# Two-layer hybrid decoder trunk on one Trainium2 core: the 512-column matmuls of the values and of the gate's v half are written as two of 256 columns

## The chip, the cores and the metric

The kernel is one program on one core of a Trainium2 chip. The core has a matrix engine (TensorE, PE in the profile, with its weight loads shown apart as PEld), a vector engine (VectorE, DVE), a scalar engine (ScalarE, ACT), GpSimd (POOL) and SyncE (SP), which here issues the weight DMAs. The time is device microseconds (us) of the whole program on that core; one profiled execution beside the timed runs gives the trace.

## What is computed

Two layers on 256 positions of width 2048, in fp32. Cut to what matters here:

```python
for l in range(DEPTH):                                  # 2 layers
    z = rms_norm(x, norm1_g[l]) @ w_in[l]               # 2048 -> 5120
    q, k, v, gu, gv = split(z)                          # 1024 columns each
    attn = dilated_attention(rotary(q), rotary(k), v)   # 8 heads
    gm = chunked_gmlp(gelu(gu), gelu(gv), ...)          # 8 groups, chunk 128
    x = x + concat(attn, gm) @ w_out[l]                 # 2048 -> 2048
    x = x + square(relu(rms_norm(x, norm2_g[l]) @ w_up[l])) @ w_down[l]   # 2048 -> 8192 -> 2048
return rms_norm(x, final_g)
```

The values `v` and the gate's v half `gv` are the two parts of `z` that the change touches: 2 layers x 2 parts x 1024 columns.

## The kernel before

Activations and weights are fp32. Each is split into a high part, rounded to the reduced fp32 type (`fp32r`), and a low part, the rest, and each product is made of three matmuls: high by high, high by low, low by high. `hs` holds the activations after the norm's gain, both parts, with the model's columns on the partitions and the 256 positions along the free axis. Weights come in pieces (`Sub`) of 128 x 1024 fp32 (512 KB): SP loads `raw` (6 buffers), ACT makes `hi` (L160, 7 buffers), DVE makes `lo` (L170, 6 buffers).

Three functions make the matmuls.

- `transposed` (L361 to L396) makes q, k, the gate's u half, the output projection, the up projection and three quarters and more of the down projection. The stationary operand is a 128 x 128 block of weights, the moving one is 256 columns (positions) of activations. Three lines: L391 (hi by high), L393 (lo by high), L395 (hi by low). A piece is 24 matmuls.
- `fast` (L398 to L431) makes the other part of the down projection by a seven-product scheme on 2 x 2 blocks. Here the stationary operand is a 128 x 128 block of activations, the moving one is 256 columns of weights: L420, L422, L423. A step makes six products (36 matmuls) and leaves the seventh (6 matmuls) in `left_over`, which the next piece of `transposed` runs after its first three matmuls (L386).
- `natural` (L433 to L452) makes `v` and `gv`. The stationary operand is a 128 x 128 block of activations, the moving one is 512 columns of weights, and the sum over the 16 blocks of the model width fills two whole PSUM banks, one for each half of the positions (`tt`). Lines L449 (xh by hi), L450 (xh by lo), L451 (xl by hi). A piece is 12 matmuls (2 blocks of rows, 2 halves of positions, 3 products); 8 pieces make 512 columns, and two such groups make a stage of 192 matmuls. There are four stages, two in each layer: the values are the layer's first stage, and the gate's v half stands between q/k and the gate's u half. In all 768 matmuls.

After a group of 512 columns, `after_v` has ACT copy the two banks out with the norm's factor (L540); `after_gv` has ACT scale them (L636) and starts the gelu.

The order is written by hand. A loop (L901 to L921) goes through `steps`: ahead of each step's matmuls it issues the ACT and DVE work for pieces two to six steps ahead and the loads, and after them it takes work from a queue (`later`, `soon`, `hook`). Some of that work is small fp32 matmuls or transposes on PE (L305, L313, L518, L573 to L580, L606, L619, L621, L675, L778), which so stand between the matmuls of a stage.

Of the kernel before, what the change touches and what calls it, by code (L numbers as in the profile page):

```python
# [39 lines left out]
KC = D // P  # L40
# [45 lines left out]
def trunk(ctx: ExitStack, tc: tile.TileContext, layout, xT, consts, gains, w, b_sp, w_sp, out):  # L86
# [10 lines left out]
    vec, act, pe = nc.vector, nc.scalar, nc.tensor  # L97
# [29 lines left out]
    def acc_bank(i=None, of=4):  # L127

        if i is None:
            i = bank_at[0] = (bank_at[0] + 1) % of  # L130
        return pacc.tile([P, 512], F32, name=f"acc{i}", tag=f"acc{i}")
# [301 lines left out]
    def natural(name, l, col0, ncols, after):  # L433

        for c in range(0, ncols, 512):
            acc = [None]
            for k0 in range(0, KC, 2):
                wt = Sub(name, l, k0 * P, col0 + c, 2, 512)

                def mm(wt=wt, k0=k0, acc=acc):  # L440
                    if k0 == 0:
                        acc[0] = [acc_bank(), acc_bank()]
                    for k in range(2):
                        for tt in range(2):
                            xh = hs[:, k0 + k, 0, tt * P:(tt + 1) * P]
                            xl = hs[:, k0 + k, 1, tt * P:(tt + 1) * P]
                            hi, lo = wt.hi[:, k, :], wt.lo[:, k, :]
                            ps = acc[0][tt]
                            pe.matmul(ps, lhsT=xh, rhs=hi, start=(k0 + k == 0), stop=False)  # L449
                            pe.matmul(ps, lhsT=xh, rhs=lo, start=False, stop=False)  # L450
                            pe.matmul(ps, lhsT=xl, rhs=hi, start=False, stop=(k0 + k == KC - 1))  # L451
                steps.append((wt, mm, (lambda c=c, acc=acc: after(c, acc[0])) if k0 + 2 == KC else None))  # L452

    def mark(fn):
# [470 lines left out]
    n = norms[-1]  # L925
# [3 lines left out]
    for c, w in [(0, 1), (1, 1)] + [(c, 2) for c in range(2, KC, 2)]:  # L929
        r = slice(c, c + w)  # L930
# [38 lines left out]
```

## Time and profile before

| what | value |
|---|---|
| timed runs | 2041.94, 2041.50, 2038.93 us; median 2041.5 us |
| the profiled execution | 2041.88 us, of which the span of its instructions is 2040.1 us |
| PE busy | 2025.8 us (99%), 16914 matmuls |
| PEld busy | 1988.5 us (97%), 16914 weight loads |
| DVE busy | 1584.5 us (78%) |
| ACT busy | 1052.6 us (52%) |
| mean granted TensorE clock | 0.997 of full |

The profile's times are of one execution. A matmul's shown duration is longer than the time to the next one's start, since matmuls are pipelined: what a stream of them costs is the distance between starts, read from the timeline as (last start minus first start) / (number of steps between).

### The profile page before, as it was taken

The page shows a single profiled execution, that of the slowest core. Times are in us where ns is not written, and L with a number is a line of the kernel's source. Part 1 is how long each engine was busy: PE and PEld are TensorE (multiplying, and loading weights), DVE is VectorE, ACT ScalarE, POOL GpSimd, SP SyncE. Part 2 cuts the span into 40 slices and gives each one's busy share as a digit, 9 for nine tenths or more (in the row PEclk, how much of TensorE's full clock was granted, in tenths as well). Part 3 has the DMA queues.
Part 4 walks back from the last instruction along what each step waited for, and adds up shares of the span by engine and source line. Part 5 has one row for each costly group of instructions (what it writes and reads, how often), then busy time and mean ns, then how long its engine had stood idle before and what let it go on. Part 6 is the DMA issues. An engine that isn't in the chain of part 4 may idle for free.

```text
span 2040.1 us, 40532 instructions
## 1 busy us (share of the span) xinstructions
PE 2025.8 (99%) x16914; PEld 1988.5 (97%) x16914; DVE 1584.5 (78%) x1970; ACT 1052.6 (52%) x1325; POOL 68.7 (3%) x90
## 2 busy tenths in 40 slices
PE   9999999999999999999999999999999999999997
PEld 8998999999999999999989989999999999999997
DVE  7666766798888888888865667668988888888886
ACT  7565444455545455444644654544554544545444
POOL 0002300000000000000000032000000000000000
PEclk9999999999999999999999999999999999999998
DMA  8545555465565655645564455554655565556553
GB/s 318 189 166 167 186 191 201 166 218 190 195 225 167 217 196 197 217 158 215 185 232 163 166 186 187 186 198 165 209 201 200 207 207 186 199 195 212 194 191 108
DMA packets 112120, 395.39 MB, mean 194 GB/s; under 512 B 12352, under 2 KB 16448, under 8 KB 111936
## 3 DMA queue, kind: packets, MB, share of 16 engines
q1 hardware_dynamic: 110800, 389.86, 56.0%
q8 instruction: 132, 2.16, 0.4%
q10 hardware_dynamic: 1136, 2.94, 0.4%
q14 instruction: 52, 0.43, 0.1%
HBM read 390.65 MB, written 2.10 MB: 193 GB/s over the span
## 4 chain that ended last, share of the span: by engine, by line
PE 98%; DVE 2%; DMA 0%; ACT 0%; issue 0%; DVEq 0%; ACTq 0%
PE acc L393 24%; PE acc L391 24%; PE acc L395 24%; PE acc L449 3%; PE acc L451 3%; PE acc L450 3%; PE aux L422 3%; PE aux L423 3%; PE aux L420 3%; PE acc L423 2%; PE acc L422 2%; PE acc L420 2%; DVE lo L170 1%; PE aux L675 0%; PE aux L619 0%; PE aux L577 0%
## 5 line engine op out<-in xcount | busy, mean ns | idle before, releaser
L160 ACT ACTIVATE hi<-raw 128x1024 fp32r<-128x1024 f32 (+1 forms) x801 | 808.0, 1047 | 473.4 <-DVE raw L214 202.0
L170 DVE TENSOR_TENSOR lo<-raw,hi 128x1024 fp32r<-128x1024 f32 (+1 forms) x801 | 944.9, 1215 | 48.7 <-ACT hi L160 33.0
L391 PE MATMUL acc<-hs,hi 128*128 128x256 f32 x2816 | 781.1, 277 | 0.0
L393 PE MATMUL acc<-hs,lo 128*128 128x256 f32 x2816 | 778.5, 276 | 0.0
L395 PE MATMUL acc<-hs,hi 128*128 128x256 f32 x2816 | 778.3, 276 | 0.0
L391 PEld LDWEIGHTS acc<-hs,hi 128*128 128x128 f32 x2816 | 529.0, 188 | 0.4 <-issue 0.2
L393 PEld LDWEIGHTS acc<-hs,lo 128*128 128x128 f32 x2816 | 528.8, 188 | 0.6 <-issue 0.2
L395 PEld LDWEIGHTS acc<-hs,hi 128*128 128x128 f32 x2816 | 528.6, 188 | 0.0
L391 PE MATMUL acc<-half,hi 128*128 128x256 f32 x1600 | 442.7, 277 | 0.0
L395 PE MATMUL acc<-half,hi 128*128 128x256 f32 x1600 | 442.2, 276 | 0.0
L393 PE MATMUL acc<-half,lo 128*128 128x256 f32 x1600 | 442.2, 276 | 0.0
L391 PEld LDWEIGHTS acc<-half,hi 128*128 128x128 f32 x1600 | 300.8, 188 | 0.0
L393 PEld LDWEIGHTS acc<-half,lo 128*128 128x128 f32 x1600 | 300.4, 188 | 0.0
L395 PEld LDWEIGHTS acc<-half,hi 128*128 128x128 f32 x1600 | 300.3, 188 | 0.0
L629 ACT ACTIVATE half<-ar 128x512 fp32r<-128x512 f32 x72 | 45.6, 634 | 190.0 <-DVE ar L734 175.4
L489 DVE TENSOR_TENSOR x<-x,acc 128x512 f32<-128x512 f32 (+1 forms) x89 | 60.3, 677 | 68.7 <-PE acc L395 68.6
L733 DVE TENSOR_TENSOR ar<-acc,nR 128x512 f32<-128x512 f32 x64 | 44.1, 689 | 86.9 <-PE acc L395 86.9
L449 PE MATMUL acc<-hi,hs 128*128 128x512 f32 x256 | 101.5, 396 | 0.7 <-ACT hs L277 0.7
L451 PE MATMUL acc<-hi,hs 128*128 128x512 f32 x256 | 100.5, 393 | 0.0
L450 PE MATMUL acc<-lo,hs 128*128 128x512 f32 x256 | 100.1, 391 | 0.0
L630 DVE TENSOR_TENSOR half<-ar,half 128x512 fp32r<-128x512 f32 x72 | 49.9, 692 | 50.4 <-ACT half L629 50.4
L277 ACT ACTIVATE hs<-x,cols 128x256 fp32r<-128x256 f32 x64 | 29.0, 501 | 91.5 <-DVE x L489 90.3
(150 smaller groups left out, 2251.8 us busy)
## 6 DMA issues: line engine op xcount, KB each, us to landing
raw<-in_w SPq DMA_DIRECT2D x731, 512.0 KB, 4.6
raw<-in_w SPq DMA_DIRECT2D x10, 256.0 KB, 5.2
x<-in_xT SPq DMA_DIRECT2D x7, 256.0 KB, 5.6
out<-x SPq DMA_DIRECT2D x7, 256.0 KB, 3.1
shared<-in_b_sp ACTq DMA_DIRECT2D x2, 512.0 KB, 8.2
shared<-in_w_sp ACTq DMA_DIRECT2D x2, 512.0 KB, 10.4
con<-in_consts ACTq DMA_DIRECT2D x1, 512.0 KB, 7.5
x<-in_xT ACTq DMA_DIRECT2D x1, 256.0 KB, 4.2
```

Of the source, the lines that this page charges most:

```text
L160: act.activation(self.h[:, j * m:(j + 1) * m], self.raw[:, j * m:(j + 1) * m], AF.Copy)
L170: vec.tensor_tensor(lo[:, r], self.raw[:, r], self.h[:, r].bitcast(F32), op=OP.subtract)
L391: pe.matmul(o, lhsT=hi, rhs=xs[:, 0, :], start=(k0 + k == 0 and (two or cb == 0)), stop=False, skip_group_check=True)
L393: pe.matmul(o, lhsT=wt.lo[:, k, cb * P:(cb + 1) * P], rhs=xs[:, 0, :], start=False, stop=False, skip_group_check=True)
L395: pe.matmul(o, lhsT=hi, rhs=xs[:, 1, :], start=False, stop=last, skip_group_check=True)
L420: pe.matmul(o[n], lhsT=xh, rhs=hi, start=(p == 0 and k == 0 and n in fresh), stop=False, skip_group_check=True)
L422: pe.matmul(o[n], lhsT=xh, rhs=lo, start=False, stop=False, skip_group_check=True)
L423: pe.matmul(o[n], lhsT=xl, rhs=hi, start=False, stop=(last and p == 1 and k == 1), skip_group_check=True)
L449: pe.matmul(ps, lhsT=xh, rhs=hi, start=(k0 + k == 0), stop=False)
L450: pe.matmul(ps, lhsT=xh, rhs=lo, start=False, stop=False)
L451: pe.matmul(ps, lhsT=xl, rhs=hi, start=False, stop=(k0 + k == KC - 1))
L489: vec.tensor_tensor(xj, xj, ps[j][:, 0:S] if alone else pair(ps)[:, j, :], op=OP.add)
```

## The change

In `natural` the three matmuls of a block become six: each product is made for the columns 0 to 255 and then for the columns 256 to 511 of the same banks, with the same stationary operand.

```diff
-                            hi, lo = wt.hi[:, k, :], wt.lo[:, k, :]
-                            ps = acc[0][tt]
-                            pe.matmul(ps, lhsT=xh, rhs=hi, start=(k0 + k == 0), stop=False)
-                            pe.matmul(ps, lhsT=xh, rhs=lo, start=False, stop=False)
-                            pe.matmul(ps, lhsT=xl, rhs=hi, start=False, stop=(k0 + k == KC - 1))
+                            for xp, wp_, n in ((xh, wt.hi, 0), (xh, wt.lo, 1), (xl, wt.hi, 2)):
+                                for h in range(2):
+                                    r = slice(256 * h, 256 * h + 256)
+                                    pe.matmul(acc[0][tt][:, r], lhsT=xp, rhs=wp_[:, k, r],
+                                              start=(k0 + k == 0 and n == 0 and h == 0),
+                                              stop=(k0 + k == KC - 1 and n == 2), skip_group_check=True)
```

On PE, at the first block of rows of the first stage, before (rows are source line, operation, the PSUM bank written, the operands read, the shape written):

```order
L449 MATMUL acc_165<-hi,hs 128x512
L450 MATMUL acc_165<-lo,hs 128x512
L451 MATMUL acc_165<-hi,hs 128x512
L449 MATMUL acc_166<-hi,hs 128x512
L450 MATMUL acc_166<-lo,hs 128x512
L451 MATMUL acc_166<-hi,hs 128x512
```

On PE at the same place now, all six products from the one line L450:

```order
L450 MATMUL acc_165<-hi,hs 128x256 x2
L450 MATMUL acc_165<-lo,hs 128x256 x2
L450 MATMUL acc_165<-hi,hs 128x256 x2
L450 MATMUL acc_166<-hi,hs 128x256 x2
L450 MATMUL acc_166<-lo,hs 128x256 x2
L450 MATMUL acc_166<-hi,hs 128x256 x2
```

The products stand in the same order, each as a pair, and the 768 matmuls of the four stages become 1536; each has a weight load of its own, as before. On PE at the end of the first layer's gate v half, where the stage hands over to `transposed` (the gate's u half), now:

```order
L450 MATMUL acc_2171<-lo,hs 128x256 x2
L450 MATMUL acc_2171<-hi,hs 128x256 x2
L391 MATMUL acc_2462<-hs,hi 128x256
L393 MATMUL acc_2462<-hs,lo 128x256
L395 MATMUL acc_2462<-hs,hi 128x256
```

The hand-over is direct, as it was: no other PE instruction stands between the stage's last matmul and L391. The order on DVE, ACT, POOL and SP is unchanged.

## Rows read from the trace of the kernel before

**Rows 1.** Page, parts 1 and 2: engines, then 40 slices of the span

```profile
PE 2025.8 (99%) x16914; PEld 1988.5 (97%) x16914; DVE 1584.5 (78%) x1970; ACT 1052.6 (52%) x1325; POOL 68.7 (3%) x90
...
PEclk9999999999999999999999999999999999999998
```

**Rows 2.** Page, part 4: the chain that ended last, by engine

```profile
PE 98%; DVE 2%; DMA 0%; ACT 0%; issue 0%; DVEq 0%; ACTq 0%
```

**Rows 3.** Groups by line and shape: busy us, mean ns | idle before, releasers

```profile
L449 PE MATMUL acc<-hi,hs 128*128 128x512 f32 x256 | 101.5, 396 | 0.7 <-ACT hs L277 0.7
L451 PE MATMUL acc<-hi,hs 128*128 128x512 f32 x256 | 100.5, 393 | 0.0
L450 PE MATMUL acc<-lo,hs 128*128 128x512 f32 x256 | 100.1, 391 | 0.0
...
L450 PEld LDWEIGHTS acc<-lo,hs 128*128 128x128 f32 x256 | 48.1, 188 | 10.6 <-issue 0.2 <-DVE lo L170 0.2
```

**Rows 4.** By stretch: us, busy PE, PEld, DVE, ACT, POOL (x instructions), PEclk, DMA, GB/s

```profile
59.40:78.44 19.04, 19.04 (x170) 19.04 (x169) 11.46 (x16) 8.31 (x10) 0.00 (x0) 1.00 0.51 166
17.20:39.18 21.98, 21.98 (x98) 18.03 (x97) 20.60 (x23) 19.08 (x26) 2.42 (x1) 1.00 0.93 362
```

**Rows 5.** Timeline of PE, ends of a stretch of 512 columns: start us, us

```profile
17.20 0.39 PE L449 MATMUL acc<-hi,hs 128*128 128x512 f32 x1
...
39.18 0.39 PE L449 MATMUL acc<-hi,hs 128*128 128x512 f32 x1
```

**Rows 6.** Timeline of PE, L420 to L423 between L391 to L395

```profile
396.21 0.28 PE L420 MATMUL aux<-hi,half 128*128 128x256 f32 x1
...
400.30 0.28 PE L391 MATMUL acc<-hs,hi 128*128 128x256 f32 x1
...
401.36 0.28 PE L391 MATMUL acc<-hs,hi 128*128 128x256 f32 x1
```

**Rows 7.** Timeline of PE, the same hand-overs in another place

```profile
937.50 0.28 PE L420 MATMUL aux<-hi,half 128*128 128x256 f32 x1
...
941.74 0.28 PE L391 MATMUL acc<-hs,hi 128*128 128x256 f32 x1
...
942.77 0.28 PE L391 MATMUL acc<-hs,hi 128*128 128x256 f32 x1
```

**Rows 8.** A stretch of the first layer's down projection, columns as in Rows 4

```profile
917.50:989.30 71.80, 71.80 (x613) 71.80 (x612) 60.94 (x72) 36.81 (x44) 0.00 (x0) 1.00 0.57 200
```

**Rows 9.** Timeline of PE, L420 to L423 after fp32 transposes

```profile
911.55 0.55 PE L778 MATMUL acc<-con,ar 128*128 128x128 f32 x3 [0.61 <-DVE ar L768]
911.85 0.36 PE L420 MATMUL aux<-hi,half 128*128 128x256 f32 x1
912.05 0.28 PE L422 MATMUL aux<-lo,half 128*128 128x256 f32 x1
912.17 0.28 PE L423 MATMUL aux<-hi,half 128*128 128x256 f32 x1
912.29 0.28 PE L420 MATMUL aux<-hi,half 128*128 128x256 f32 x1
912.40 0.28 PE L422 MATMUL aux<-lo,half 128*128 128x256 f32 x1
912.52 0.28 PE L423 MATMUL aux<-hi,half 128*128 128x256 f32 x1
```

**Rows 10.** Timeline of PE, restarts after fp32 matmuls, at 512 and at 256 columns

```profile
42.73 0.48 PE L449 MATMUL acc<-hi,hs 128*128 128x512 f32 x1
43.05 0.40 PE L450 MATMUL acc<-lo,hs 128*128 128x512 f32 x1
...
212.42 0.37 PE L391 MATMUL acc<-hs,hi 128*128 128x256 f32 x1
212.62 0.28 PE L393 MATMUL acc<-hs,lo 128*128 128x256 f32 x1
212.74 0.28 PE L395 MATMUL acc<-hs,hi 128*128 128x256 f32 x1
```

**Rows 11.** L449 alone, in the four stages after their first fp32 interruption

```profile
42.73:51.06 8.33, 4.82 (x12) 2.23 (x12) 1.00 0.64 214
157.44:197.98 40.54, 22.20 (x56) 10.50 (x56) 1.00 0.58 193
1029.26:1064.49 35.23, 19.37 (x48) 9.00 (x48) 1.00 0.71 240
1168.68:1209.20 40.52, 22.20 (x56) 10.51 (x56) 1.00 0.56 193
```

**Rows 12.** Busy time after direct hand-overs from L451 to L391, columns as in Rows 4

```profile
198.50:211.00 12.50, 12.50 (x113) 12.50 (x112) 10.49 (x26) 7.42 (x9) 5.08 (x6) 1.00 0.47 144
1064.50:1091.50 27.00, 27.00 (x240) 26.99 (x239) 13.80 (x15) 13.33 (x16) 0.00 (x0) 1.00 0.46 154
```

## The prediction

> **What bounds the kernel now.** I read the engines' shares first, then the chain of waits, then the timeline of PE. PE is busy 99% of the span, and its clock digit is 9 in all slices but the last [rows 1]; the chain that ended last is PE for 98% and nothing else over 2% [rows 2]. So the time is the sum of the distances between PE's instructions, and an edit on PE is priced by what it does to these distances. In the touched stages PE's idle time is 0.7 us in all 768 matmuls [rows 3]: neither weights nor banks are late there. DVE is the nearest engine, 20.60 of 21.98 us busy in the first values stage, and PE still idles nowhere [rows 4]; elsewhere DVE has more room.
>
> The shown durations (some 393 ns for 512 columns) overlap, so I go by starts. In the first values stage 96 matmuls of 512 columns (8 pieces of 12) take from 17.20 to 39.18, 21.98 us or **228.96 ns each** [rows 5]. In q and k 168 matmuls of 256 columns (7 pieces of 24) take the 19.04 us of the stretch from 59.40 to 78.44, **113.33 ns each**; both stretches have the granted clock at 1.00, the 2.4 GHz level [rows 4]. Two of 256 are 226.67 ns, so a pair would be 2.29 ns shorter than the matmul that it replaces.
>
> But 256 columns have a second price. `fast`, with the operand roles of `natural` (activations stationary, weights moving), runs 36 matmuls from 396.21 to 400.30 (113.6 ns each), and then, over the hand-over to three matmuls of `transposed` and the six left over, 9 take 1.06 us, **117.8 ns each** [rows 6]. At another hand-over it is the other way round: 36 take 4.24 us (117.8) and the next 9 take 1.03 us (114.4) [rows 7]. So there is a short and a long rhythm, 4.4 ns apart. A stream keeps the one that it is in, and the hand-over from the `fast` form to the `transposed` form changes it: short to long in the first place, long to short in the second. In the stretch from 917.50 to 989.30 most of the 613 matmuls are in the long one: 71.80/613 is 117.1 ns [rows 8].
>
> **The change part by part.**
>
> *768 matmuls become 768 pairs.* All lie on the path. In the short rhythm: 768 x (2 x 113.33 - 228.96) = 768 x (-2.29) = **-1.8 us**. In the long one: 768 x (2 x 117.8 - 228.96) = 768 x 6.6 = **+5.1 us**. These are the two bounds. I take the short one: it is the price of the longest unbroken run of 256 columns that I read, the 168 of q and k.
>
> *768 more weight loads.* A load is shown as 188 ns and lies beside a matmul [rows 3]. The load unit goes from 18.03 of 21.98 us busy to the 19.04 of 19.04 that q and k show [rows 4]. Their 113.33 ns is thus a price with a load for each matmul in it, and nothing comes on top. That both halves use the same stationary operand saves nothing: L449 and L450 share theirs today, and L450 has all its 256 loads at 188 ns [rows 3].
>
> The Trainium skill, page "TensorE: Matmul & The Clock Gate", section "Back-to-back issue gap", gives the distance of warm matmuls as N/2.4 plus 2.5 ns, a fixed price for each, which speaks against any split: as an estimate, 768 x 2.5 = +1.9 us, and 2043.4 us without the hand-over price. The trace disagrees for these operands: if 512 columns are twice a stream time plus a fixed part, and 256 once, the fixed part is 2 x 113.33 - 228.96 = -2.3 ns in the short rhythm and +6.6 ns in the long one.
>
> *Restarts.* Ten times a small fp32 group stands between a stage's matmuls. The first matmul after it takes longer: 320 ns against 229 at 512 columns, 200 against 113 at 256 [rows 10], 91 and 87 more. No difference is counted: 10 x 4 ns.
>
> *The hand-over to `transposed`.* Three of the stages end directly before L391 (both gate v halves, and the second layer's values; the first layer's values end before a small fp32 group). If the new form acts as `fast` does, a stream that comes in short goes on long [rows 6] until the next fp32 group. After the first gate v half that is the 113 matmuls of the stretch from 198.50, and as many in the second layer; after the second values 240 [rows 12]. Today these run at the short price (27.00 us for 240 counted). 466 x 4.4 ns = **+2.1 us**; the other bound is 0.
>
> *Waits and other engines.* The wait for `hi` stays on the first matmul of a piece, that for `lo` on the first of the lo product, and the last read of each buffer is at the same place in the piece, so ACT and DVE get their buffers back as before. The banks are complete one matmul start plus a shorter matmul later: the pair's second half starts 113 ns after the first and ends where the old one ended, within some ns. Cost nothing either way; ACT's copies run beside later matmuls. Nothing moves on the DMA queue.
>
> Sum: -1.8 + 2.1 = +0.3 us. On the profiled execution's 2041.88 us (span 2040.1 and 1.8 us around it) that is 2042.2; the profiled execution lies 0.4 us over the median of the runs, 2041.5, and I predict against the median: **2041.8 us**.
>
> **The rivals.**
>
> *The gain stays, no hand-over price.* For it: today's hand-overs from L451 to L391 do not leave the long rhythm behind [rows 12]. Against: they are of 512 columns. -1.8: 2039.7 us.
>
> *Long after each restart.* After the fp32 transposes that end at 911.85, `fast` goes on at (912.52 - 912.05)/4 = 117.5 ns [rows 9]; q, k and the u half fall back to the short rhythm in three matmuls [rows 10]. `natural` has the operand roles of `fast`. L449 has 12 + 56 + 48 + 56 = 172 matmuls after the first restart of their stages [rows 11], so 3 x 172 = 516 pairs would be long and 252 short: 516 x 6.6 - 252 x 2.3 = +2.8 us, with no hand-over price, since a long stream comes out short [rows 7]: 2044.3 us.
>
> *The other side: each half pays its own start.* The long rhythm holds in all four stages, from the first matmul on, because the alternation of two halves of a bank, or of two loads of one operand, is what the long rhythm is. Nothing in the trace alternates so; that is for it, and that `fast` goes through two to six groups of outputs within a run at one price is against it [rows 6]. +5.1: 2046.6 us, 0.25% slower. The page's fixed price, above, is this rival at 2.5 ns a pair. It decides from a pair of 234.3 ns on (0.2% is 4.1 us, 5.3 ns in each of 768 pairs).
>
> *The slow stretch is lost.* Which rhythm a stretch has depends on how it was entered, and the change shifts what comes before. If the stretch from 917.50 runs short after, 613 x (117.1 - 113.3) = 2.3 us go, with the -1.8 of the first rival 4.1 in all: 2037.4 us. The lowest run of before, 2038.93, is 2.6 us under the median, which would fit such a spread.
>
> *The change does nothing.* Had a repeated load or a repeated bank its price hidden, a pair would be 229 ns: 2041.5 us. The rows of 256 columns leave little room for it.
>
> **How the numbers follow.** Forecast 0.38; gain without the hand-over price 0.20; long after restarts 0.20; each half pays 0.12; slow stretch lost 0.05; nothing 0.05. The range reaches from 2038.5 (below the gain's 2039.7, with half of the slow stretch's 2.3 us) to 2045.5 (above the restarts' 2044.3, under the 2046.6) and leaves out some 0.17. A measurement of this kernel tells about 0.2%, 4.1 us, from no change: slower is the one case of 2046.6, 0.12; faster is the slow stretch's and a little of the first rival's, 0.05; the rest, 0.83, is within.
>
> **What would show it.** In the timeline of after, the distance between starts of L450: 113.3 or 117.8 ns, before and behind each restart; the distances of L391 to L395 behind the three direct hand-overs; the mean distance in the down projection's slow stretch; L450's count of 1536 and as many loads. The prediction is wrong if PE idles in these stages, if a pair costs over 234 ns, or if a rhythm changes in a stage that the diff does not touch.

## The result and the profile after

The changed kernel takes **2044.03 us** (median of 12 runs, 2042.44 to 2048.76) against 2041.91 us (2038.65 to 2044.98) for the kernel before in the same comparison: ratio **1.0018**, 95% interval 1.001 to 1.0026, that is +3.7 us (+2.0 to +5.3). The ratio is not that of the two medians, which are 2.1 us apart: the executions of each kernel fall into groups some 2.5 us apart (below), and a median depends on how many fall into which. It is slower by 0.1 to 0.3%. The forecast was 2041.8 us, no difference; the time is inside the range, the direction was not foreseen as the likeliest, and it is nearly the 2044.3 us of the rival "long after each restart".

The page of after, engines, as in [rows 1]:

```profile
PE 2027.1 (99%) x17682; PEld 2021.8 (99%) x17682; DVE 1583.6 (78%) x1970; ACT 1052.1 (52%) x1325; POOL 64.0 (3%) x90
```

768 matmuls and 768 loads more, PE as full as before, and the load unit now as full as PE. DVE and ACT are busy as long as before, within 1 us.

The timeline of PE, after, gives for the touched stages what [rows 5 and 6] give for the kernel before (start us, us; rows that read alike are merged, their number stands behind the x). First the second layer's values up to the first small fp32 group, then the first gate v half behind a group, then its last part and the hand-over to L391:

```profile
1016.71 0.39 PE L450 MATMUL acc<-hi,hs 128*128 128x256 f32 x2
...
1027.59 0.28 PE L305 MATMUL aux<-ones,nacc 128*128 128x1 f32 x2
```

```profile
158.37 0.48 PE L450 MATMUL acc<-hi,hs 128*128 128x256 f32 x2
158.69 0.40 PE L450 MATMUL acc<-lo,hs 128*128 128x256 f32 x2
...
169.76 0.82 PE L607 MATMUL aux<-con,ar 128*128 128x128 f32 x6
...
177.62 0.40 PE L450 MATMUL acc<-lo,hs 128*128 128x256 f32 x2
...
200.00 0.29 PE L391 MATMUL acc<-hs,hi 128*128 128x256 f32 x1
```

96 matmuls from 1016.71 to 1027.59 are 113.3 ns each, the short rhythm. Behind the group that ends at 158.37, the last 94 of four pieces' 96 matmuls take 11.07 us, 117.8 ns each; from 177.62 to 200.00 190 take 22.38 us, again 117.8. In the three later stages that is the whole picture: 113.3 ns up to the first stop of PE's stream (a point where the next matmul starts late, behind an fp32 group or in a wait), 117.8 ns from there to the stage's end; and behind all ten fp32 groups of the four stages the rhythm is long. In the first stage PE also waits for its operands. It starts late twice at the very beginning (6.07 to 6.66) and yet goes on in the short rhythm: the 140 matmuls from 6.66 to 22.53 take 15.87 us, 113.4 ns each. At 23.03 it waits for `lo`. ACT had waited 1.48 us for the load of a piece, DVE 1.31 us for ACT, and DVE's `lo` ends at 22.97. From this wait on the rhythm is long. Timelines of ACT, of DVE and of PE:

```profile
19.46 1.06 ACT L160 ACTIVATE hi<-raw 128x1024 fp32r<-128x1024 f32 x1 [1.48 <-DMA raw<-in_w]
```

```profile
20.95 0.89 DVE L281 SCALAR_TENSOR_TENSOR hs<-x,cols,hs 128x256 fp32r<-128x256 f32 x2 [1.31 <-ACT hs L277]
21.75 1.22 DVE L170 TENSOR_TENSOR lo<-raw,hi 128x1024 fp32r<-128x1024 f32 x1
```

```profile
6.07 0.75 PE L450 MATMUL acc<-hi,hs 128*128 128x256 f32 x2
6.66 0.39 PE L450 MATMUL acc<-lo,hs 128*128 128x256 f32 x2
...
22.53 0.62 PE L450 MATMUL acc<-hi,hs 128*128 128x256 f32 x4
23.03 0.51 PE L450 MATMUL acc<-lo,hs 128*128 128x256 f32 x2
```

From the stage's first matmul to the instruction behind its last one, read from the two timelines (the fp32 groups inside are the same):

| stage | before | after |
|---|---|---|
| first layer, values | 5.99 to 51.08: 45.09 us | 6.07 to 52.06: 45.99 us |
| first layer, gate v half | 149.41 to 197.99: 48.58 us | 150.39 to 200.00: 49.61 us |
| second layer, values | 1017.46 to 1064.50: 47.04 us | 1016.71 to 1064.57: 47.86 us |
| second layer, gate v half | 1160.65 to 1209.24: 48.59 us | 1160.70 to 1210.31: 49.61 us |
| sum | 189.30 us | 193.07 us, **+3.8** |

The profiled execution of after is nevertheless only 0.6 us longer than that of before (2042.44 against 2041.88 us), mostly because a stretch that the change does not touch came out short in it: from the end of the first gate v half to the second values it takes 816.71 us against 819.47, 2.8 us less (behind the last touched stage it is another 0.5 us less). First the busy time of the stretch of [rows 8], after; then, by the timeline, L391 to L395 behind the second values, as in [rows 12]:

```profile
917.50:989.30 71.80, 71.80 (x634) 71.80 (x633) 63.15 (x74) 39.04 (x46) 0.00 (x0) 1.00 0.60 209
```

```profile
1064.57 0.28 PE L391 MATMUL acc<-hs,hi 128*128 128x256 f32 x1
...
1091.78 0.38 PE L574 MATMUL aux<-con,ones 128*128 128x128 f32 x2
```

The same 71.80 us hold 634 matmuls instead of 613: 21 more, 2.4 us. And 240 matmuls behind the second values take 27.21 us, 113.4 ns each: no price at this hand-over.

### The profile page after: what moved, and what is told of

The parts are those of the page before. It is cut to its first block, busy times and chain, and to the rows that moved or that the text cites. A ratio compares the mean times of both kernels' runs of the same rounds, so it can differ in the third digit from the quotient of the medians.

```text
span 2040.6 us, 42062 instructions
## 1 busy us (share of the span) xinstructions
PE 2027.1 (99%) x17682; PEld 2021.8 (99%) x17682; DVE 1583.6 (78%) x1970; ACT 1052.1 (52%) x1325; POOL 64.0 (3%) x90
## 4 chain that ended last, share of the span: by engine, by line
PE 98%; DVE 2%; issue 0%; ACT 0%; DVEq 0%
PE acc L391 24%; PE acc L393 24%; PE acc L395 24%; PE acc L450 9%; PE aux L422 3%; PE aux L423 3%; PE aux L420 3%; PE acc L423 2%; PE acc L422 2%; PE acc L420 2%; DVE lo L170 1%; PE aux L676 0%; PE aux L578 0%; PE aux L620 0%; PE aux L607 0%; PE aux L893 0%
## 5 line engine op out<-in xcount | busy, mean ns | idle before, releaser
L391 PE MATMUL acc<-hs,hi 128*128 128x256 f32 x2816 | 780.7, 277 | 0.0
L393 PE MATMUL acc<-hs,lo 128*128 128x256 f32 x2816 | 778.1, 276 | 0.0
L395 PE MATMUL acc<-hs,hi 128*128 128x256 f32 x2816 | 777.9, 276 | 0.0
L393 PEld LDWEIGHTS acc<-hs,lo 128*128 128x128 f32 x2816 | 528.7, 188 | 0.4 <-issue 0.2
L391 PEld LDWEIGHTS acc<-hs,hi 128*128 128x128 f32 x2816 | 528.6, 188 | 0.2 <-issue 0.2
L395 PEld LDWEIGHTS acc<-hs,hi 128*128 128x128 f32 x2816 | 528.5, 188 | 0.0
L391 PE MATMUL acc<-half,hi 128*128 128x256 f32 x1600 | 442.2, 276 | 0.0
L395 PE MATMUL acc<-half,hi 128*128 128x256 f32 x1600 | 441.7, 276 | 0.0
L393 PE MATMUL acc<-half,lo 128*128 128x256 f32 x1600 | 441.7, 276 | 0.0
L391 PEld LDWEIGHTS acc<-half,hi 128*128 128x128 f32 x1600 | 300.3, 188 | 0.0
L393 PEld LDWEIGHTS acc<-half,lo 128*128 128x128 f32 x1600 | 300.3, 188 | 0.0
L395 PEld LDWEIGHTS acc<-half,hi 128*128 128x128 f32 x1600 | 300.3, 188 | 0.0
L450 PE MATMUL acc<-hi,hs 128*128 128x256 f32 x1024 | 164.8, 280 | 0.0
L450 PEld LDWEIGHTS acc<-hi,hs 128*128 128x128 f32 x1024 | 139.0, 188 | 0.7 <-ACT hs L277 0.3
L450 PE MATMUL acc<-lo,hs 128*128 128x256 f32 x512 | 101.3, 279 | 0.0
L450 PEld LDWEIGHTS acc<-lo,hs 128*128 128x128 f32 x512 | 78.0, 188 | 0.1
```

The source lines that it names most:

```text
L391: pe.matmul(o, lhsT=hi, rhs=xs[:, 0, :], start=(k0 + k == 0 and (two or cb == 0)), stop=False, skip_group_check=True)
L393: pe.matmul(o, lhsT=wt.lo[:, k, cb * P:(cb + 1) * P], rhs=xs[:, 0, :], start=False, stop=False, skip_group_check=True)
L395: pe.matmul(o, lhsT=hi, rhs=xs[:, 1, :], start=False, stop=last, skip_group_check=True)
L450: pe.matmul(acc[0][tt][:, r], lhsT=xp, rhs=wp_[:, k, r], start=(k0 + k == 0 and n == 0 and h == 0), stop=(k0 + k == KC - 1 and n == 2), sk ...
```

## The experiments

**The changed kernel once more, and its six matmuls in two other orders.** Is it the stop that makes the rhythm long, or the form of the pairs? `again` is the changed kernel. `order_half` makes all three products of one half before the other:

```diff
-                            for xp, wp_, n in ((xh, wt.hi, 0), (xh, wt.lo, 1), (xl, wt.hi, 2)):
-                                for h in range(2):
-                                    r = slice(256 * h, 256 * h + 256)
+                            for h in range(2):
+                                r = slice(256 * h, 256 * h + 256)
+                                for xp, wp_, n in ((xh, wt.hi, 0), (xh, wt.lo, 1), (xl, wt.hi, 2)):
```

`order_tt` puts the two halves of the positions innermost:

```diff
+                        for i, w_, n in ((0, wt.hi, 0), (0, wt.lo, 1), (1, wt.hi, 2)):
+                            for h in range(2):
+                                r = slice(256 * h, 256 * h + 256)
+                                for tt in range(2):
+                                    xp = hs[:, k0 + k, i, tt * P:(tt + 1) * P]
```

> The changed kernel once more, for a second look at its trace. Theory A (a stream of matmuls with stationary activations comes out of a stop of PE in the long rhythm, 117.8 ns between starts, and keeps it; a stream that was never stopped stays at 113.3): the 516 pairs behind the first small fp32 group of each stage are again at 235.5 ns a pair, the first two pieces of each gate v half and the first four of the second values stage again at 226.7. Theory B (the rhythm is drawn anew in each execution, like a coin): some of these groups change sides. Both: the down projection's stretch of the first layer from 917 to 989 us, at 117.1 ns in the trace of before and at 113.4 in that of after, may come out either way. Time 2042 to 2046 us.

> The six matmuls of a block in another order: all three products of the columns 0 to 255, then all three of 256 to 511, which is the order of the lines L420 to L423 of the down projection (one half of a bank three times in a row, the same stationary operand twice instead of four times in a row). Theory A (a stop sets the long rhythm, whatever the order): as the changed kernel, 117.8 ns behind each small fp32 group, 113.3 ahead of the first one in the gate v halves, 2044 us. Theory C (the alternation of the two halves of a bank is the long rhythm): 113.3 ns in all four stages, 768 x 6.6 x 516/768 = 3.4 us less than the changed kernel's stages, 2040 to 2041 us.

> The twelve matmuls of a block of rows in another order, the two halves of the positions innermost, so that no stationary operand is loaded twice in a row and the bank changes with each matmul. Theory A (a stop sets the long rhythm): as the changed kernel, 117.8 ns behind each small fp32 group, 2044 us. Theory D (loading the same stationary operand again is what makes the long rhythm, as in the lines L420 and L422, which share theirs too): 113.3 ns behind the groups as well, like q and k, whose stationary operand changes with each matmul; then 768 pairs x -2.3 ns against the kernel before, 2040 us, or 2041 to 2042 with a long rhythm handed to the following stage.

Measured: `again` 2042.99 us; `order_half` 2043.18 us, ratio to the kernel before 1.0013 (0.9998 to 1.0028); `order_tt` 2043.36 us, 1.0019 (1.001 to 1.0028). The gate v half behind its first group, timelines of `order_half` and of `order_tt`:

```profile
159.14 0.28 PE L450 MATMUL acc<-lo,hs 128*128 128x256 f32 x1
...
170.34 0.38 PE L607 MATMUL aux<-con,ar 128*128 128x128 f32 x2
```

```profile
158.81 0.60 PE L449 MATMUL acc<-hi,hs 128*128 128x256 f32 x3
...
170.21 0.38 PE L606 MATMUL aux<-con,ar 128*128 128x128 f32 x2
```

95 matmuls in 11.20 us and, less the 0.20 us of the first, 95 in 11.20 us: 117.9 ns in both orders. The three later stages last 49.60, 47.85 and 49.60 us in each of the three kernels, as in the changed one. Theories B, C and D fall for these stages: nothing is drawn by lot there, neither order of the pairs takes the long rhythm away, and its start is at the group each time. In the first stage, where the stops are waits, theory A does not hold as it stands. That stage differs from execution to execution: 45.99 us in the changed kernel's first trace, 46.22 in `again`, 46.51 in `order_half` and 46.39 in `order_tt`. The first two come short out of the late starts at the beginning and turn long at a later wait, the two others are long from the first piece on.

The trace of `order_tt` came with the slow stretch (613 matmuls from 917.50 to 989.30) and its execution took 2046.16 us, against 2042.97 for that of `order_half`, which has 634 there.

**One stop more.** A small fp32 group behind the second piece of the second layer's values, in a place that had been short in every trace:

```diff
+        def stop_here():
+            spare = aux_bank()
+            for h in range(2):
+                pe.matmul(spare[:, h * P:(h + 1) * P], lhsT=ones, rhs=ident, start=(h == 0), stop=True,
+                          skip_group_check=True)
+        if l:
+            hook(base + 1, stop_here)
```

> The changed kernel with one more small fp32 group, two matmuls of 128 columns on constants, put behind the second piece of the second layer's values, a place where the stream ran at 113.3 ns in each look so far. Theory A (a stop of PE's stream sets the long rhythm): the two pieces behind it, 48 matmuls, go at 117.8 ns, the two ahead stay at 113.3. Theory E (what stands in those places, the waits for the norm's factor or the buffers of the later pieces, sets it): 113.3 ns in all four. Total 2042 to 2046 us; the added group costs some 0.4 us.

Timeline of PE:

```profile
1036.36 0.39 PE L450 MATMUL acc<-hi,hs 128*128 128x256 f32 x2
...
1041.81 0.61 PE L710 MATMUL aux<-con,ones 128*128 128x128 f32 x4
1042.17 0.48 PE L450 MATMUL acc<-hi,hs 128*128 128x256 f32 x2
1042.49 0.40 PE L450 MATMUL acc<-lo,hs 128*128 128x256 f32 x2
...
1047.91 0.39 PE L305 MATMUL aux<-ones,nacc 128*128 128x1 f32 x3
```

48 matmuls ahead of the group in 5.45 us, 113.5 ns; behind it the last 46 of 48 in 5.42 us, 117.8 ns. So the added group set the long rhythm, in one place and one execution, and theory E falls. Whether it is the interruption or the group's own fp32 matmuls that does it, this run does not tell apart; the wait at 23.03 above has no fp32 matmul in it. The time was not as expected, 2064.27 us, and it is not the added group: in this execution the first layer's whole down projection ran long, busy time by stretch:

```profile
454.00:1008.00 554.00, 553.62 (x4704) 553.19 (x4703) 453.67 (x525) 270.86 (x304) 0.00 (x0) 1.00 0.55 191
```

553.62/4702 is 117.7 ns a matmul (the count less two under way at the left edge), 4.4 ns over the short rhythm, some 20 us in all. The code there is the same. The timeline of PE shows where it began, at an L393 that starts late:

```profile
436.25 0.28 PE L391 MATMUL acc<-hs,hi 128*128 128x256 f32 x1
436.44 0.38 PE L393 MATMUL acc<-hs,lo 128*128 128x256 f32 x1
436.65 0.28 PE L395 MATMUL acc<-hs,hi 128*128 128x256 f32 x1
```

The starts are 0.19 and 0.21 us apart. In the first trace of the changed kernel the same L393 starts late too (435.80, 435.97, 436.19: 0.17 and 0.22 us), and `transposed` goes on short behind it. The same wait left one rhythm in the one execution and the other in the other; why was not tried.

**No stops inside the gate v halves.** One line ahead of each:

```diff
+        mark(flush)
         natural("w_in", l, 4 * AW, AW, after_gv)
```

> The changed kernel with all queued attention work run out ahead of each gate v half, so that no small fp32 group stands inside these two stages (PE stands still there for it, some 5 to 15 us in each layer; the total is not the question). Theory A: all 192 pairs of each gate v half at the rhythm of their entry, and no change inside. If PE has been stopped just ahead of the stage, the entry is a stop and the rhythm is long from the first pair on, 235.5 ns; if the stream of q and k runs into the stage, it is short, 226.7 ns. And what follows: a stage that ends short hands the long rhythm to the gate's u half (117.8 ns in L391 to L395 up to the next small group), one that ends long hands it the short one (113.3). Theory C or D (the form of the stage makes the rhythm): the stage goes long by itself, wherever it starts.

2065.64 us, with PE standing for the attention work ahead of each stage. The entry is a stop, and the 384 matmuls behind it are long; the first layer's gate v half by stretch, and what follows by timeline:

```profile
165.10:209.90 44.80, 44.80 (x383) 44.80 (x382) 24.29 (x37) 20.65 (x22) 9.79 (x18) 1.00 0.57 188
```

```profile
210.17 0.28 PE L391 MATMUL acc<-hs,hi 128*128 128x256 f32 x1
...
223.78 0.60 PE L676 MATMUL aux<-shared 128*128 128x128 f32 x4
```

44.80/381 is 117.6 ns; behind the hand-over 120 matmuls take 13.61 us, 113.4 ns. A stage that ends long comes out short, as theory A had it. That the stage is long from its entry, theories C and D say as well; against them stand the 24 short pairs that open this stage in the changed kernel, with the same form.

**512 columns behind the stop.** Does a stream of 512 columns lead back into the short rhythm? `mixed` keeps 512 columns in the first block of each piece (`k == 0`) and makes pairs in the second. `first512` keeps them only in the first block behind each group and in the first half of the first stage:

```diff
+        stops = {(0, 2): (8, 13), (1, 2): (4, 7, 9)}.get((l, col0 // AW), (2, 6, 8))
+        wide = lambda c, k0, k: (c // 64 + k0 // 2 in stops and k == 0) or (l == 0 and col0 == 2 * AW and c == 0)
-                                for h in range(2):
-                                    r = slice(256 * h, 256 * h + 256)
+                                for h in range(1 if wide(c, k0, k) else 2):
+                                    r = slice(0, 512) if wide(c, k0, k) else slice(256 * h, 256 * h + 256)
```

> Every second block of rows (the first of each piece) keeps its matmuls of 512 columns, the other is made in pairs of 256: 384 matmuls of 512 and 768 of 256, so each stream of pairs is entered from six matmuls of 512 and none directly from a stop. Theory A1 (a stop leaves the long rhythm, and matmuls of 512 lead into the short one, as they do today at the hand-over to L391): 256 columns at 113.3 ns behind the small fp32 groups too; 384 x -2.3 ns = -0.9 us against the kernel before, and where a stage ends short, 117.8 ns in L391 to L395 behind it, +2 us. Theory A2 (matmuls of 512 carry the rhythm of their entry on unseen): 117.8 ns behind the groups, 113.3 ahead of them, about half of the changed kernel's loss, +2 us.

> The changed kernel, with 512 columns kept only in the first block of rows behind each small fp32 group and in the first half of the first stage (where PE waits for the loads); 666 or so of the 768 products are pairs. Theory A1 (512 columns lead into the short rhythm): nearly all pairs at 226.7 ns, stages 1.3 to 1.5 us shorter than before; if a stage that ends short hands the long rhythm on, 2.1 us go again in L391 to L395. Theory A2 (they carry the rhythm of their entry): 235.5 ns behind the groups as in the changed kernel, +3 us against before.

`mixed`: 2042.69 us, ratio 1.0005 (0.9996 to 1.0014). `first512`: 2041.52 us, ratio 0.9999 (0.9981 to 1.0017). Neither theory, A1 (512 columns lead into the short rhythm) or A2 (they carry the rhythm of their entry on), is wholly right. In `mixed`'s first stage the pairs between the blocks of 512 columns go at 117.8 ns from the start to the end, so 512 columns can carry a rhythm on unseen; behind the groups of the three later stages its pairs are short in seven places of nine. In `first512` the pairs behind ten such blocks are short in eight places, and long in two, the last part of both gate v halves. The two long places of `mixed` in the later stages are the same two, which speaks for the place and against a draw. Timeline of `first512`, there:

```profile
158.56 0.62 PE L451 MATMUL acc<-hi,hs 128*128 128x512 f32 x3
159.02 0.39 PE L451 MATMUL acc<-lo,hs 128*128 128x256 f32 x2
...
168.32 0.49 PE L608 MATMUL aux<-con,ar 128*128 128x128 f32 x3
...
177.37 0.40 PE L451 MATMUL acc<-lo,hs 128*128 128x256 f32 x2
...
198.34 0.29 PE L391 MATMUL acc<-hs,hi 128*128 128x256 f32 x1
```

82 matmuls from 159.02 in 9.30 us are 113.4 ns; 178 from 177.37 in 20.97 us are 117.8. Behind a stop a block of 512 columns mostly, not always, leaves the short rhythm. And both kernels have what the changed one lacks, a second values stage that ends short. Timelines of `mixed`, of `first512`:

```profile
1062.87 0.28 PE L391 MATMUL acc<-hs,hi 128*128 128x256 f32 x1
...
1091.13 0.60 PE L574 MATMUL aux<-con,ones 128*128 128x128 f32 x4
```

```profile
1061.72 0.28 PE L391 MATMUL acc<-hs,hi 128*128 128x256 f32 x1
...
1090.00 0.38 PE L575 MATMUL aux<-con,ones 128*128 128x128 f32 x2
```

28.26 and 28.28 us for the 240 matmuls that take 27.21 in the changed kernel: 117.8 ns, +1.1 us. The hand-over price of the prediction exists, behind a stage that ends short.

**Four matmuls of 128 columns.** Is it the columns that limit a matmul of 256?

```diff
-                                for h in range(2):
-                                    r = slice(256 * h, 256 * h + 256)
+                                for h in range(4):
+                                    r = slice(128 * h, 128 * h + 128)
```

> The same 768 products as four matmuls of 128 columns each, 3072 in all, each with a load of 128 x 128 weights. Theory L (at 256 columns the weight load, not the columns, sets the distance: 113.3 ns is a load's price): still 113 to 118 ns for each matmul of 128 columns, 453 to 471 ns a product against 229, that is +172 to +186 us, 2213 to 2228 us. Theory M (the columns set it, and the load is hidden): some 57 to 65 ns each, 2040 to 2065 us.

2246.94 us, +205. Busy time of a stretch of the first gate v half at a granted clock of 1.00:

```profile
220.00:252.00 32.00, 32.00 (x289) 32.00 (x289) 9.45 (x11) 10.55 (x21) 0.00 (x0) 1.00 0.30 99
```

32.00/287 is 111.5 ns for half the columns, so theory M falls: the columns do not set this distance. That the weight load sets it, as theory L says, fits the load unit's 32.00 of 32.00 us, but it is not shown: each matmul here has a load, and any other price of 111 ns a matmul would look the same. By theory L 256 columns stand just over the load's price (113.3), with nothing to hide a load that comes late, while 512 columns stand at twice it; that this is why two rhythms exist is a guess. (The time is over the expected 2228 us because the granted clock fell in parts of this kernel, to 0.68 of full on average from 1113.50 to 1180.00. Why it fell there was not tried.)

**The kernel before, twice.** Most runs of the kernel before fall into two groups, 2038.6 to 2039.9 and 2041.3 to 2042.8 us; a few lie at 2044.3 to 2045.0.

> The kernel before, unchanged, for a second look at its trace. The four stages stand in 177.3 us of distances between starts, whatever the execution (matmuls of 512 columns have one price). The runs of this kernel fall into two groups, 2038.6 to 2039.6 and 2041.3 to 2042.8 us. Theory S: the groups differ by the first layer's stretch around 917 to 997 us: an execution of the lower group has it at 113.3 ns, some 2.6 to 3.2 us shorter, one of the upper group at 117.1 ns. Theory U: the groups differ elsewhere (the loads at the start, waits on DVE), and the stretch is as slow in both.

> The same again, so that both groups of times are likelier to be seen with a trace. Theory S: the time of an execution and the price of its stretch from 917 to 997 us go together. Theory U: they don't.

2041.79 and 2039.33 us. The stretch, in the one and in the other:

```profile
917.50:989.30 71.80, 71.80 (x613) 71.80 (x612) 60.94 (x72) 36.80 (x44) 0.00 (x0) 1.00 0.57 199
```

```profile
917.50:989.30 71.80, 71.80 (x634) 71.80 (x633) 63.08 (x74) 39.03 (x46) 0.00 (x0) 1.00 0.61 209
```

The slower execution has the slow stretch, the faster one does not: theory S, by one execution of each kind here and the two of the pair orders above. The difference of 2.5 us is the size of the effect under study, which is why medians of few runs mislead here. Traces of the same kind compare better. Without the slow stretch the changed kernel took 2042.44 and 2042.99 us and `order_half` 2042.97, against 2039.33: +3.1 to +3.7. With it `order_tt` took 2046.16 us, against 2041.88 and 2041.79: +4.3. That is the stages' +3.8 again, while the two traces compared first, 2042.44 and 2041.88, are of different kinds.

**A version with neither loss.** `first512`, with 512 columns also in the second half of each gate v half and in the last block of the second values; 420 of 768 products are pairs.

```diff
-        stops = {(0, 2): (8, 13), (1, 2): (4, 7, 9)}.get((l, col0 // AW), (2, 6, 8))
-        wide = lambda c, k0, k: (c // 64 + k0 // 2 in stops and k == 0) or (l == 0 and col0 == 2 * AW and c == 0)
+        stops = {(0, 2): (8, 13), (1, 2): (4, 7, 9, 15)}.get((l, col0 // AW), (2, 6))
+        wide = lambda c, k0, k: ((c // 64 + k0 // 2 in stops and k == (c // 64 + k0 // 2 == 15)) or
+                                 (l == 0 and col0 == 2 * AW and c == 0) or (col0 == 4 * AW and c == 512))
```

> As first512 (pairs of 256 columns, with one block of 512 columns behind each small fp32 group), but 512 columns as well in the second half of each gate v half, where the pairs of first512 went at 117.8 ns, and in the last block of the second layer's values, so that each stage hands over to L391 from 512 columns: 420 of the 768 products are pairs. If each stretch of pairs is short, 420 x -2.3 ns = -1.0 us in the stages against before (176.4 us instead of 177.3), and L391 to L395 behind the second values at 113.3 ns again: 2040.5 us against a median of 2041.5, within 0.2%. If the pairs go long somewhere, up to 420 x 6.6 = +2.8 us.

2039.24 us against 2039.85, ratio 0.9995 (0.9985 to 1.0004): no difference that a measurement can tell. Timeline, the second values and what follows:

```profile
1064.14 0.28 PE L391 MATMUL acc<-hs,hi 128*128 128x256 f32 x1
...
1091.37 0.49 PE L576 MATMUL aux<-con,ones 128*128 128x128 f32 x3
```

All pairs are short, and the 240 matmuls behind take 27.23 us. The three later stages last 48.40, 46.67 and 48.40 us, 0.7 us less in all than before; the first one, where PE waits for loads, 45.25 against 45.09. Most of the gain that the arithmetic promised is there, and far under what a measurement can tell. (The execution that left this trace took 2044.08 us: it had the slow stretch in both layers' down projections.)

## Why the prediction was wrong

*What bounds the kernel* held: PE's starts are the time, and DVE, ACT and the queue kept out of it.

*768 pairs* is the step that failed. It priced both rhythms rightly (113.3 and 117.8 ns, found again within 0.1 ns) and then chose the short one for all pairs, because q and k have it. The rows that spoke for this case were [rows 9]: activations as the stationary operand, a stop ahead, long. Of 768 pairs 168 are short in the trace of after (72, 24, 48 and 24 in the four stages) and 96 in that of `order_half`; the others are long. The term was set at -1.8 us and measured **+3.8**. The bound of +5.1 was not reached, since the stretches ahead of the first stop are short. The rival "long after each restart" had the mechanism and 2044.3 us. Of its 516 long and 252 short pairs 480 and 96 are in the three later stages: 480 x 6.6 - 96 x 2.3 = +2.9 us, and they show +2.9 (147.08 - 144.21). For the first stage that leaves -0.1 us, and it shows +0.9: the rival counted fp32 groups alone, and there a wait for operands set the long rhythm too, though not each wait did. That 2044.3 lies so near the median of 2044.03 us is in part luck, since the medians move with the slow stretch. That the time lies inside the forecast's range is no merit of the sum either: the range was drawn to hold this rival.

*768 more loads* at no price of their own: right in the sum, since 113.3 contains a load. But "nothing comes on top" passed over what `quarters` shows, that with a load for each matmul 128 columns cost 111.5 ns, nearly what 256 do.

*Restarts*, 0: right for the first matmul alone, which takes some 200 ns behind a group against 113, as much more as at 512 columns (87 and 91 ns). What the restart does to the matmuls behind it was priced at nothing, and that is the loss.

*The hand-over*, +2.1: measured 0. The mechanism is right (+1.1 us behind the second values in `mixed` and `first512`, where +1.1 was worked out), but it hangs on the failed step: a stage that ends long comes out short.

*The slow stretch* as a rival: right about what it is, a rhythm set by the entry, and wrong to tie it to the change. It comes and goes in the unchanged kernel too, so the sign that the prediction named for being wrong, a rhythm that changes where the diff does not reach, says nothing about the change here.

*Each half pays its own start*, the rival on the other side: neither alternation nor repetition is needed for the long rhythm, by the two orders of the pairs, and a pair in the short one is cheaper than 512 columns, not dearer. No rhythm shows the 2.5 ns a matmul that the prediction quoted. The Trainium skill, page "TensorE: Matmul & The Clock Gate", section "Back-to-back issue gap", calls the formula that of an isolated matmul and says that in a stream of loads and matmuls both set the distance, which the prediction left out. `quarters` agrees as far as it goes: 128 columns cost nearly what 256 do.

The forecast came out near zero because the gain and the hand-over price both hang on this one choice, with opposite signs. Had the pairs been priced by the rows nearest in form, the forecast would have been the rival's.

What stays open: why an fp32 group leaves streams with stationary activations in the long rhythm (all ten groups of the touched stages in the trace of after) and `transposed` mostly in the short one (28 of the 30 places in the same trace where it goes on for more than three matmuls behind such a group), which of the two a block of 512 columns leads into, and why the same wait now and then puts a whole layer's down projection into the long one.

## What to carry to other kernels

Where a kernel's time is the distance between matmul starts, read that distance in several places before pricing a change of shape, and take the row whose operand roles and entry are those of the changed place, not the longest clean one. In this kernel a stop in front of matmuls of 256 columns can cost 4% of all that follow (117.8 against 113.3 ns), while the 512 columns before the change paid for a stop once. And if two groups of run times are as far apart as the effect that is looked for, find out first what separates them.

## What the runs showed that was not expected

A matmul of 128 columns costs 111.5 ns, one of 256 113.3 or 117.8, one of 512 229: with a weight load for each, halving 256 columns saves 2 ns. A rhythm of 256 columns can last for hundreds of matmuls. It flips where stationary activations hand over to stationary weights (113.3 to 117.8 and back, in `natural` and in `fast`), and a stop can set it anew; one execution went through 554 us of unchanged code mostly in the long one, 20 us. Behind a stop, one block of 512 columns brought the following pairs into the short rhythm in seven of ten places in `mixed`, eight of ten in `first512` and all eight in `wide_ends`.
